# Retention readout scales computed with tokens on partitions and spread by TensorE, and weights prepared three units ahead in layer 0

## Chip, cores and metric

One core of one Trainium2 chip runs the whole network in one program. The metric is the device time of one execution in microseconds (us), lower is better. Engines are named as in the profile: PE is the matrix engine (TensorE), DVE the vector engine (VectorE), ACT the scalar engine (ScalarE), POOL is GpSimd, SP issues most transfers (SyncE).

## What is computed

A two-layer backbone over 512 tokens (256 context tokens, 256 latent tokens), model width 1024, all in float32. Layer 0 is a four-head bidirectional retention mixer followed by a gated convolutional feed-forward block; layer 1 is an RG-LRU mixer with the same kind of feed-forward block. What the change touches is the readout of one retention head:

```
def head_groupnorm(y, gain):
    mu = mean(y, axis=-1);  var = mean((y - mu)**2, axis=-1)      # over the head's 512 value columns
    return (y - mu) * rsqrt(var + EPS) * gain

def readout(y, g):
    return (silu(g) * head_groupnorm(y, gn)) @ w_out
```

So each head needs one scale per token: 512 numbers 1/sqrt(var + eps).

## The kernel before, in words

**Layout.** Activations lie transposed: a tile has 128 features on the partitions and the 512 tokens in its columns. A head's value output is four tiles `av` (128 of the 512 value columns each), left in PSUM; the means are already taken out. A scale per token therefore has to multiply the columns of a tile, and stands in every partition of a 128x512 tile.

**Matrix products.** Each float32 product is made of three faster ones (`mm3`, lines 522 to 524): both operands are split into a high and a low part, and high times high, high times low, low times high are added up in PSUM. For a weight block the parts are `whi` and `wlo`, for an activation they are for instance `zhi` and `zlo`.

**Weights.** All weight blocks (128x128) stand in one stream in the order of their use, cut in units of eight blocks. A unit arrives as `raw` (one transfer of 512 KB, nine buffers), ACT rounds it to `whi` (line 420), DVE subtracts to make `wlo` (line 452). When the first block of unit u is about to be used, `blk` calls `prep_units(u + ahead)`: it issues the low parts up to unit u + ahead and the high parts up to unit u + ahead + 1, never more than five units (WBUFS) beyond the current one. `self.ahead` is 1, then 2 while `start` runs, stays 2 through the retention layer and the first feed-forward block, and is set to 3 where `lru` begins. Some units hold weights for layer 1, which are split early and written back to DRAM (`pre`, line 471 and 479; `kept`, the transfers on ACT's queue), or matrices of the modulation: ACT multiplies them by a strip (`ada`, `adap`, lines 576 and 579) and POOL adds the products up (line 580).

**What sets the order.** Each engine does its instructions in the order in which the program records them. Some work is recorded late on purpose: `defer` puts pieces in a queue, `tick(n)` records the next n of them between two products, `flush` all of them; `lag` records the low part of a split one split later.

**A head.** For head h: four products for q and k, each followed by the rotation `rope_split` (lines 902 to 907: one copy on ACT, five instructions on DVE); for heads 1 and 2 then `ret_out(h-1)`, the output product of the head before (units of `ret_out` weights); a gate product; the scores; v (`ret_v`: per 128 tokens a mean `vm`, then `vhi` by ACT at line 961 and `vlo` by DVE at line 962); more gate products; `ret_av`, which leaves the four `av` tiles and `gacc`, the sum of their squares (`gsq`); then the readout. `ret_stats` makes the scale: one product of a tile of ones with `gacc` sums over the partitions and leaves the variance in all of them (`gst`, 128x512), ACT takes the square root (`sd`), DVE the reciprocal (`rstd`, line 679). `ret_z` makes four tiles z = av * gain * scale * silu(g) (`zt`, lines 1007 and 1008) and splits them (`zhi` on ACT, line 544, `zlo` on DVE, line 545), in five deferred pieces. For head 0 `ret_stats` stands after the first q/k product of head 1, for the others ahead of the last gate product. So the readout of heads 0, 1 and 2 is made while the q/k products of the next head run, and that of head 3 while `ret_out(2)` runs.

Of the kernel before, what the change touches and what calls it, by code (L numbers as in the profile page):

```python
# [7 lines left out]
F32 = mybir.dt.float32  # L8
F32R = mybir.dt.float32r
AF = mybir.ActivationFunctionType  # L10
ALU = mybir.AluOpType

P = 128
D = 1024
KD = D // P
NT = 512
# [40 lines left out]
def qk_cols(h):  # L57
    return [2 * h, 2 * h + 1, 8 + 2 * h, 8 + 2 * h + 1]
# [128 lines left out]
class Buf:  # L187


    def __init__(self, kind="s"):  # L190
        self.kind, self.n, self.t = kind, 0, None
# [105 lines left out]
class Net:  # L297
    def __init__(self, ctx, tc, wpk, xt, cv, par, cst, out):
        self.tc, self.nc, self.out = tc, tc.nc, out
        self.d_w, self.d_x, self.d_c, self.d_par, self.d_cst = wpk, xt, cv, par, cst  # L300
        self.cp = ctx.enter_context(tc.tile_pool(name="cp", bufs=1))
        self.wp = ctx.enter_context(tc.tile_pool(name="wp", bufs=WBUFS))
        self.gp = ctx.enter_context(tc.tile_pool(name="gp", bufs=1))
        self.pp = ctx.enter_context(tc.tile_pool(name="pp", bufs=8, space=bass.MemoryType.PSUM))
        self.nslot = 54
        self.uid = 0
        self.raw, self.units = {}, {}
        self.nload = self.nunit = self.nlo = self.pos = self.npast = 0
        self.held, self.ahead, self.spread, self.umode = None, 0, "A", {}
        self.auto = True  # L310
        self.piece_of = {p[1] // 16: i for i, p in enumerate(PIECES) if p[0] == "blk"}
        self.bg, self.lagq, self.due, self.now = deque(), deque(), [], 0
        self.ada_ps, self.ada_acc, self.adaq, self.ada_rate = {}, {}, deque(), 4
        self.ada_done, self.ada_sum = set(), {}
        self.preq, self.keepq = deque(), deque()
        self.dp = ctx.enter_context(tc.tile_pool(name="dp", bufs=1, space=bass.MemoryType.DRAM))
        self.kept = {}

# [674 lines left out]
        self.gacc = acc  # L993

    def ret_stats(self):
        ps = self.ps(name="gst")
        self.nc.tensor.matmul(ps, self.ones_v, self.gacc, start=True, stop=True)
        self.grs = self.rstd_of(ps, NT)

    def ret_z(self, h):  # L1000

        nc = self.nc
        zs, av, sg, rs = [], self.av, self.avsg, self.grs

        def first(c):
            t = self.slot(name="zt")
            nc.vector.scalar_tensor_tensor(t, av[c], self.pc("gn", 4 * h + c), rs, ALU.mult, ALU.mult)  # L1007
            nc.vector.tensor_tensor(t, t, sg[c], ALU.mult)
            hi = self.slot(dt=F32R, name="zhi")
            lo = self.slot(dt=F32R, name="zlo")  # L1010
            return t, hi, lo

        def step(c):
            if c:
                t, hi, lo = prev.pop()
                self.split(t, hi, lo)
                zs.append((hi, lo))
            if c < 4:
                prev.append(first(c))

        prev = []
        self.defer(*[lambda c=c: step(c) for c in range(5)])
        return zs

    def ret_out(self, h, zs):
# [89 lines left out]
    def retention(self):  # L1115
        self.hpos = {}
        self.setup()
        a = self.const([P, KD, 2], name="amul")
        hl = {}
        pss = self.start(a, hl)  # L1120
        zs = None
        for h in range(HEADS):
            self.sg = []
            if h == 0:
                qk = [self.rope_split(pss[j], j % 2) for j in range(4)]
                self.silu_g(pss[4])
                self.silu_g(pss[5])
                self.ret_g(h, hl, 2)
                self.decay(0)
            else:  # L1130
                qk = []
                for j, c in enumerate(qk_cols(h)):
                    ps = self.gemm("ret_in", range(KD), c, lambda k: [(0, hl[k])], NT)
                    if h == 1 and j == 0:
                        self.ret_stats()
                        zs = self.ret_z(0)
                    self.tick(2)
                    qk.append(self.rope_split(ps, j % 2))
                self.flush()
                if h < 3:  # L1140
                    self.ret_out(h - 1, zs)
                else:
                    zprev = zs
                self.ret_g(h, hl, 0)
            self.qk = (qk[:2], qk[2:])
            if h == 0:
                self.ret_v(h, hl)
                self.flush()
                self.ret_scores()
                self.ret_g(h, hl, 3)  # L1150
                self.ret_av()
                self.decay(1)
            else:
                self.flush()
                self.ret_scores()
                self.ret_v(h, hl)
                self.ret_g(h, hl, 1)
                self.ret_av()
                self.ret_g(h, hl, 2)
                if h < 3:  # L1160
                    self.decay(h + 1)
            if h:
                self.ret_stats()
                self.ret_g(h, hl, 3)
                zs = self.ret_z(h)
        self.ret_out(2, zprev)
        self.flush()
        self.need("f0")
        self.stats_begin()
        a = self.make_amul(self.const([P, KD, 2], name="amul"), 0, "norm_ffn")  # L1170
        for m in range(2):
            ps = self.gemm("ret_out", range(12, 16), m, lambda k: [(0, zs[k - 12])], NT)
            for s in range(2):
                self.residual(ps[:, s * NS:(s + 1) * NS], 0, 2, m, s)
                self.stats_add(m, s)
        self.hl = {}
        dst = lambda k, s: [t[:, s * NS:(s + 1) * NS] for t in self.hwide(k, self.hl)]
        return self.staged_out("ret_out", range(12, 16), range(2, KD), lambda k: zs[k - 12], 0, 2,
                               lambda s: self.norm_steps(0, "norm_ffn", a, s, dst))
# [611 lines left out]
```

## Time and profile before

| | |
|---|---|
| Device time, three runs | 1222.65, 1226.3, 1227.6 us (median 1226.3) |
| The profiled execution's own time | 1223.15 us |
| Span of its program in the trace | 1221.4 us |
| PE busy | 1186.3 us, 97% of the span |
| DVE, ACT, POOL busy | 892.5, 731.9, 360.0 us |
| PE idle for a low part of weights (line 452) | 18.5 us in nine times, the longest 6.0 us |

The profile is one execution. Busy PE time counts every matrix product from its issue to its modelled end, so 97% says that PE seldom has nothing to do; it does not say that its products run at full speed. The column PEclk of the views by stretch gives the clock that was granted to PE: 1.00 is 2.4 GHz, 0.50 is 1.2 GHz.

### The profile page before, as it was taken

How to read it: one execution, taken by the hardware profiler on the slowest of the kernel's cores; microseconds unless marked ns; L12 is line 12 of the kernel's file. 1: busy time of each engine (PE TensorE's matmuls, PEld its weight loads, DVE VectorE, ACT ScalarE, POOL GpSimd, SP SyncE). 2: the span in 40 equal slices, each digit the busy share in tenths (PEclk: the TensorE clock that was granted, in tenths of full speed). 3: DMA queues.
4: the chain of work that ended last, by engine and by line, in shares of the span. 5: the costliest groups of instructions: out<-in, count | busy, mean ns of one | idle time of the engine just before them, and what ended most of it. 6: DMA issues, size and time to landing. Idle time of an engine off the chain costs nothing.

```text
span 1221.4 us, 18028 instructions
## 1 busy us (share of the span) xinstructions
PE 1186.3 (97%) x6768; PEld 1010.2 (83%) x6768; DVE 892.5 (73%) x1285; ACT 731.9 (60%) x1100; POOL 360.0 (29%) x238
## 2 busy tenths in 40 slices
PE   9999799999979999999999999999999999999997
PEld 5678688778868889877878888789988788999996
DVE  5665996896596598599945676754658877988743
ACT  5465566765753545987643656542497956666542
POOL 0000555746370012798733435360000001000010
PEclk9999899999989999999999999999999999999999
DMA  9975479758566482445688645654586994655631
GB/s 334 339 253 216 182 238 318 250 193 310 208 224 212 145 319 100 143 154 191 215 313 268 222 153 203 231 196 159 162 313 204 327 333 162 193 187 183 195 107 35
DMA packets 79160, 265.38 MB, mean 217 GB/s; under 512 B 9312, under 2 KB 13024, under 8 KB 79072
## 3 DMA queue, kind: packets, MB, share of 16 engines
q1 hardware_dynamic: 66976, 221.75, 54.0%
q10 hardware_dynamic: 12096, 42.47, 8.9%
q8 instruction: 53, 0.87, 0.3%
q14 instruction: 35, 0.29, 0.1%
HBM read 219.62 MB, written 42.99 MB: 215 GB/s over the span
## 4 chain that ended last, share of the span: by engine, by line
PE 78%; DVE 12%; ACT 3%; DMA 3%; issue 2%; SPq 1%; DVEq 0%; ACTq 0%
PE ps L522 22%; PE ps L524 22%; PE ps L523 22%; DVE wlo L452 3%; PE ps L946 2%; PE ps L947 2%; PE ps L948 2%; DVE rstd L679 1%; ACT adap L579 1%; DVE fzlo L545 1%; PE av L524 1%; PE av L523 1%; PE av L522 1%; DVE zt L1007 1%; PE ps L1639 1%
## 5 line engine op out<-in xcount | busy, mean ns | idle before, releaser
L580 POOL TENSOR_TENSOR ada<-ada,adap 128x512 f32<-128x512 f32 x196 | 324.2, 1679 | 365.5 <-ACT adap L579 232.4
L524 PE MATMUL ps<-hhi,wlo 128*128 128x512 f32 (+1 forms) x640 | 245.6, 384 | 11.2 <-DVE wlo L452 11.2
L522 PE MATMUL ps<-hhi,whi 128*128 128x512 f32 (+1 forms) x640 | 248.7, 389 | 0.0
L523 PE MATMUL ps<-hlo,whi 128*128 128x512 f32 (+1 forms) x640 | 244.2, 382 | 0.0
L665 POOL TENSOR_TENSOR sq<-sq,sq 128x256 f32<-128x256 f32 x29 | 32.4, 1127 | 472.9 <-ACT sq L659 382.9
L523 PE MATMUL ps<-hx,whi 128*128 128x256 f32 x592 | 168.1, 284 | 0.4 <-DVE hx L698 0.2
L522 PE MATMUL ps<-hx,whi 128*128 128x256 f32 x592 | 168.3, 284 | 0.2 <-ACT hx L697 0.2
L524 PE MATMUL ps<-hx,wlo 128*128 128x256 f32 x592 | 167.5, 283 | 0.0
L524 PEld LDWEIGHTS ps<-hhi,wlo 128*128 128x128 f32 x640 | 121.6, 190 | 37.4 <-DVE wlo L452 14.5
L522 PEld LDWEIGHTS ps<-hhi,whi 128*128 128x128 f32 x640 | 121.7, 190 | 31.6 <-issue 6.5
L523 PEld LDWEIGHTS ps<-hlo,whi 128*128 128x128 f32 x640 | 121.7, 190 | 22.9 <-issue 1.0
L522 PEld LDWEIGHTS ps<-hx,whi 128*128 128x128 f32 x592 | 113.5, 192 | 4.2 <-issue 2.5
L523 PEld LDWEIGHTS ps<-hx,whi 128*128 128x128 f32 x592 | 113.5, 192 | 1.2 <-DVE hx L698 0.8
L524 PEld LDWEIGHTS ps<-hx,wlo 128*128 128x128 f32 x592 | 113.5, 192 | 0.0
L1190 DVE SCALAR_TENSOR_TENSOR cv<-ps,par,cv 128x510 f32<-128x510 f32 (+1 forms) x88 | 53.9, 613 | 61.7 <-ACT cv L1187 61.7
L1187 ACT ACTIVATE cv<-ps,par 128x512 f32<-128x512 f32 (+1 forms) x88 | 58.7, 670 | 65.8 <-PE ps L524 64.9
L522 PE MATMUL ps<-fzhi,whi 128*128 128x512 f32 (+1 forms) x198 | 72.7, 367 | 0.0
L524 PE MATMUL ps<-fzhi,wlo 128*128 128x512 f32 (+1 forms) x198 | 72.4, 365 | 0.0
L523 PE MATMUL ps<-fzlo,whi 128*128 128x512 f32 (+1 forms) x198 | 72.4, 365 | 0.0
L708 DVE SCALAR_TENSOR_TENSOR xc<-ps,mod,xc 128x256 f32<-128x256 f32 x48 | 23.0, 479 | 54.5 <-PE ps L524 54.4
L524 PE MATMUL ps<-zhi,wlo 128*128 128x512 f32 (+1 forms) x152 | 55.7, 366 | 7.4 <-DVE wlo L452 7.4
L1191 DVE SCALAR_TENSOR_TENSOR cv<-ps,par,cv 128x510 f32<-128x510 f32 (+1 forms) x88 | 54.2, 616 | 3.1
(791 smaller groups left out, 2786.4 us busy)
## 6 DMA issues: line engine op xcount, KB each, us to landing
kept<-pre ACTq DMA_DIRECT2D x40, 512.0 KB, 5.7
whi<-kept SPq DMA_DIRECT2D x40, 512.0 KB, 4.3
wlo<-kept SPq DMA_DIRECT2D x40, 512.0 KB, 5.5
ak<-wpk SPq DMA_DIRECT2D x32, 256.0 KB, 6.3
xc<-xt SPq DMA_DIRECT2D x4, 256.0 KB, 3.7
x<-xt SPq DMA_DIRECT2D x4, 256.0 KB, 5.2
xst<-xhi SPq DMA_DIRECT2D x16, 64.0 KB, 3.8
cst<-cst SPq DMA_DIRECT2D x3, 192.0 KB, 5.1
```

Of the source, the lines that this page charges most:

```text
L452: self.eng(e).tensor_tensor(d[q, o:n], r[q, o:n], hi[q, o:n].bitcast(F32), ALU.subtract)
L522: mm(ps, w[0], x[0], start=start, stop=False)
L523: mm(ps, w[0], x[1], start=False, stop=False)
L524: mm(ps, w[1], x[0], start=False, stop=stop)
L580: nc.gpsimd.tensor_tensor(acc[i, s], acc[i, s], t, ALU.add)
L665: nc.gpsimd.tensor_tensor(self.acc[s], self.acc[s], sq, ALU.add)
L946: mm(pss[t], xh, wh, start=k == 0, stop=False)
L947: mm(pss[t], xh, wl, start=False, stop=False)
L948: mm(pss[t], xl, wh, start=False, stop=k == KD - 1)
L1187: nc.scalar.activation(acc, ps[:, :n], AF.Identity, scale=w(1), bias=self.pc("fcb", layer * 44 + f))
L1190: nc.vector.scalar_tensor_tensor(a3[:, :, 1:], p3[:, :, :NS - 1], w(0), a3[:, :, 1:], ALU.mult, ALU.add)
L1191: nc.vector.scalar_tensor_tensor(a3[:, :, :NS - 1], p3[:, :, 1:], w(2), a3[:, :, :NS - 1], ALU.mult, ALU.add)
```

## The change

The scale of a head is made with a token per partition. Four products take a 128-token chunk of `gacc` as the stationary operand and one column of ones as the moving one, and leave the variances as 128x4; ACT's square root and DVE's reciprocal work on 128x4 (`gsd`). A new function, `spread_scale`, brings the 512 scales back into all partitions: four products take a column of `gsd`, repeated 128 times, as the stationary operand and the identity as the moving one (`gb`, 128x512 in PSUM), and ACT copies the result to SBUF (`grs`). It stands as one more deferred piece ahead of the five of `ret_z`. And `self.ahead` is set to 3 at the beginning of the head loop.

```diff
     def ret_stats(self):
-        ps = self.ps(name="gst")
-        self.nc.tensor.matmul(ps, self.ones_v, self.gacc, start=True, stop=True)
-        self.grs = self.rstd_of(ps, NT)
+        nc = self.nc
+        ps = self.ps([P, 4], name="gst")
+        for j in range(4):
+            nc.tensor.matmul(ps[:, j:j + 1], self.gacc[:, j * P:(j + 1) * P], self.ones_v[:, 0:1], start=True, stop=True)
+        self.gsd = self.gp.tile([P, 4], F32, tag="gs", name=f"gsd{self.nhead}", bufs=2)
+        nc.scalar.activation(self.gsd, ps, AF.Sqrt, bias=self.eps)
+        nc.vector.reciprocal(self.gsd, self.gsd)
+        self.nhead += 1
+
+    def spread_scale(self, sd):
+        ps = self.ps(name="gb")
+        for j in range(4):
+            self.nc.tensor.matmul(ps[:, j * P:(j + 1) * P], sd[:, j:j + 1].to_broadcast([P, P]), self.cc("ident"),
+                                  start=True, stop=True)
+        rs = self.slot(name="grs")
+        self.nc.scalar.copy(rs, ps)
+        return rs
...
-        zs, av, sg, rs = [], self.av, self.avsg, self.grs
+        zs, av, sg, sd, rs = [], self.av, self.avsg, self.gsd, []
...
-            nc.vector.scalar_tensor_tensor(t, av[c], self.pc("gn", 4 * h + c), rs, ALU.mult, ALU.mult)
+            nc.vector.scalar_tensor_tensor(t, av[c], self.pc("gn", 4 * h + c), rs[0], ALU.mult, ALU.mult)
...
-        self.defer(*[lambda c=c: step(c) for c in range(5)])
+        self.defer(lambda: rs.append(self.spread_scale(sd)), *[lambda c=c: step(c) for c in range(5)])
...
         pss = self.start(a, hl)
+        self.ahead = 3
         zs = None
         for h in range(HEADS):
```

Where the engines' orders move, at three places.

DVE before, the end of head 0's readout, during the q/k products of head 1 (rawN is a unit of weights; the last `zlo` is what `ret_out(0)` needs of its fourth block on):

```order
L906 TENSOR_TENSOR qklo_1315<-ps_1250,qkhi_1314 128x256
L907 TENSOR_TENSOR ra_1316<-ra_1316,rb_1317 128x256
L452 TENSOR_TENSOR wlo_1329<-raw24a,whi_1260 128x1024
L545 TENSOR_TENSOR zlo_1306<-zt_1302,zhi_1305 128x512
L617 TENSOR_TENSOR mod_170<-adat_1356,par_89 128x4 x4
L545 TENSOR_TENSOR zlo_1313<-zt_1309,zhi_1312 128x512
L903 TENSOR_TENSOR ra_1385<-ps_1324,cst_556 128x256
```

DVE with the change, at the same place:

```order
L453 TENSOR_TENSOR wlo_1365<-raw24b,whi_1281 128x1024
L546 TENSOR_TENSOR zlo_1338<-zt_1334,zhi_1337 128x512
L1023 SCALAR_TENSOR_TENSOR zt_1405<-av_1165,par_89,grs_1261 128x512
L1024 TENSOR_TENSOR zt_1405<-zt_1405,sg_1116 128x512
L546 TENSOR_TENSOR zlo_1345<-zt_1341,zhi_1344 128x512
L904 TENSOR_TENSOR ra_1414<-ps_1356,cst_556 128x256
L905 TENSOR_TENSOR rb_1415<-ps_1356,cst_558 64x256
L906 TENSOR_TENSOR rb_1415<-ps_1356,cst_558 64x256
L907 TENSOR_TENSOR qklo_1413<-ps_1356,qkhi_1412 128x256
L908 TENSOR_TENSOR ra_1414<-ra_1414,rb_1415 128x256
L453 TENSOR_TENSOR wlo_1427<-raw26a,whi_1363 128x1024
L546 TENSOR_TENSOR zlo_1409<-zt_1405,zhi_1408 128x512
```

Before, one rotation less and the low parts up to raw24a stood ahead of the last `zlo`; now the third rotation of head 1 and the low parts of raw24b and raw26a stand ahead of it too, while those of raw22b and raw21b have moved ahead of the first `zt`.

ACT before, the scale of head 0:

```order
L420 CAST whi_1191<-raw22b 128x1024
L677 ACT_TABLE_LOAD
L677 ACTIVATE sd_1221<-gst_1219,eps_178 128x512
L607 COPY adarow_1061<-ada_677 128x512
L471 CAST pre_1227<-raw21b 128x1024
L544 CAST zhi_1232<-zt_1229 128x512
```

ACT with the change, the scale of head 0 and its copy after the spreading:

```order
L421 CAST whi_1208<-raw24a 128x1024
L1003 ACT_TABLE_LOAD
L1003 ACTIVATE gsd_1241<-gst_1236,eps_178 128x4
L577 ACTIVATE ada_1204<-raw23a,strip_183 128x512
L577 ACTIVATE ada_1205<-raw23a,strip_183 128x512
L580 ACTIVATE adap_1246<-raw23a,strip_183 128x512
L580 ACTIVATE adap_1249<-raw23a,strip_183 128x512
L488 DMA kept_1252<-pre_1005 128x1024
L489 DMA kept_1252<-raw21a 128x1024
L1013 COPY grs_1261<-gb_1256 128x512
```

Between the square root and the copy, ACT now has four products of the modulation and two transfers to issue.

ACT before, the split of v of head 1:

```order
L961 ACTIVATE vhi_1925<-ps_1733,vm_1913 128x512
L961 ACTIVATE vhi_1928<-ps_1734,vm_1916 128x512
L961 ACTIVATE vhi_1932<-ps_1735,vm_1919 128x512
L961 ACTIVATE vhi_1936<-ps_1736,vm_1922 128x512
L471 CAST pre_1953<-raw34b 128x1024
L487 DMA kept_1956<-pre_1910 128x1024
L488 DMA kept_1956<-raw34a 128x1024
L487 DMA kept_1959<-pre_1953 128x1024
L488 DMA kept_1959<-raw34b 128x1024
L420 CAST whi_1964<-raw38a 128x1024
```

ACT with the change, at the same place:

```order
L421 CAST whi_1921<-raw38a 128x1024
L577 ACTIVATE ada_1902<-raw36a,strip_183 128x512
L577 ACTIVATE ada_1903<-raw36a,strip_183 128x512
L580 ACTIVATE adap_1951<-raw36a,strip_183 128x512
L580 ACTIVATE adap_1954<-raw36a,strip_183 128x512
L472 CAST pre_1957<-raw37a 128x1024
L962 ACTIVATE vhi_1971<-ps_1773,vm_1959 128x512
L962 ACTIVATE vhi_1974<-ps_1774,vm_1962 128x512
L962 ACTIVATE vhi_1978<-ps_1775,vm_1965 128x512
L962 ACTIVATE vhi_1982<-ps_1776,vm_1968 128x512
```

The rounding of raw38a and the work on raw36a and raw37a, which stood behind the four `vhi`, stand ahead of them.

## Rows read from the trace of the kernel before

**Rows 1.** The page, part 1: busy us, share of the span, instructions.

```profile
PE 1186.3 (97%) x6768; PEld 1010.2 (83%) x6768; DVE 892.5 (73%) x1285; ACT 731.9 (60%) x1100; POOL 360.0 (29%) x238
```

**Rows 2.** Waits of PE in 110:160, 245:255, 345:372, 500:585: total us, times, longest.

```profile
PE ps L524 <- DVE wlo L452: 6.2, 2, 6.0
...
PE ps L524 <- DVE wlo L452: 1.6, 2, 1.3
...
PE ps L524 <- DVE wlo L452: 7.0, 2, 4.0
...
PE ps L524 <- DVE wlo L452: 3.7, 3, 2.3
```

**Rows 3.** Windows: PE, PEld, DVE, ACT, POOL busy, PEclk, DMA share, GB/s.

```profile
142.00:150.00 8.00, 5.44 (x13) 4.16 (x14) 7.94 (x13) 5.34 (x10) 8.00 (x6) 0.50 0.52 183
...
152.00:160.00 8.00, 8.00 (x36) 6.30 (x35) 7.81 (x15) 3.43 (x6) 3.23 (x3) 1.00 0.47 143
...
364.00:368.00 4.00, 4.00 (x11) 3.14 (x10) 3.94 (x8) 0.32 (x2) 0.51 (x1) 0.50 0.74 256
```

**Rows 4.** Timeline of PE, products without the three-part split: start, us.

```profile
119.28 1.02 PE L997 MATMUL gst<-gsq,ones_v 128*128 128x512 f32 x2
...
131.04 0.96 PE L613 MATMUL adat<-cst,adarow 128*128 128x24 f32 x8
```

**Rows 5.** Groups of DVE by form: busy us, mean ns, idle us ahead of them.

```profile
L679 DVE RECIPROCAL rstd<-sd 128x512 f32<-128x512 f32 x4 | 13.4, 3353 | 9.3 <-ACT sd L677 9.3
...
L617 DVE TENSOR_TENSOR mod<-adat,par 128x4 f32<-128x4 f32 x32 | 2.6, 153 | 6.9 <-PE adat L613 6.8
```

**Rows 6.** Timeline of ACT and DVE, readout of head 0.

```profile
120.39 1.28 ACT L677 ACT_TABLE_LOAD   x1 [0.84 <-PE gst L997]
121.68 0.69 ACT L677 ACTIVATE sd<-gst,eps 128x512 f32<-128x512 f32 x1
...
122.40 3.35 DVE L679 RECIPROCAL rstd<-sd 128x512 f32<-128x512 f32 x1 [2.10 <-ACT sd L677]
...
126.75 0.74 DVE L1007 SCALAR_TENSOR_TENSOR zt<-av,par,rstd 128x512 f32<-128x512 f32 x1
...
129.53 0.42 DVE L903 TENSOR_TENSOR ra<-ps,cst 128x256 f32<-128x256 f32 x1
...
131.52 1.22 DVE L452 TENSOR_TENSOR wlo<-raw22b,whi 128x1024 fp32r<-128x1024 f32 x1
...
134.36 2.31 DVE L479 TENSOR_TENSOR raw21b<-raw21b,pre 128x1024 fp32r<-128x1024 f32 x1
...
142.22 2.28 DVE L452 TENSOR_TENSOR wlo<-raw24a,whi 128x1024 fp32r<-128x1024 f32 x1
...
146.39 1.49 DVE L545 TENSOR_TENSOR zlo<-zt,zhi 128x512 fp32r<-128x512 f32 x1
```

**Rows 7.** Timeline of ACT and PE, split of v of head 1.

```profile
199.64 3.05 ACT L961 ACTIVATE vhi<-ps,vm 128x512 fp32r<-128x512 f32 x4 [3.71 <-DVE vm L955]
...
206.01 0.39 PE L522 MATMUL av<-phi,vhi 128*128 128x512 f32 x1
...
209.18 1.05 ACT L420 CAST whi<-raw38a 128x1024 fp32r<-128x1024 f32 x1 [5.55 <-PE av L524]
210.13 1.33 ACT L576 ACTIVATE ada<-raw36a,strip 128x512 f32<-128x512 f32 x2
```

**Rows 8.** Timeline of DVE and PE, end of the readout of head 1.

```profile
252.19 1.29 DVE L545 TENSOR_TENSOR zlo<-zt,zhi 128x512 fp32r<-128x512 f32 x2
...
254.28 0.39 PE L523 MATMUL ps<-zlo,whi 128*128 128x512 f32 x1
```

**Rows 9.** Timeline of DVE and PE, q/k products of head 3 with the readout of head 2.

```profile
343.17 0.75 DVE L1007 SCALAR_TENSOR_TENSOR zt<-av,par,rstd 128x512 f32<-128x512 f32 x1
...
371.26 0.39 PE L522 MATMUL ps<-qkhi,qkhi 128*128 128x512 f32 x1
...
371.37 0.98 DVE L545 TENSOR_TENSOR qklo<-ra,qkhi 128x256 fp32r<-128x256 f32 x2
```

More of the change, by code (lines that the diff above doesn't have):

```diff
@@ L315, in __init__ @@
         self.preq, self.keepq = deque(), deque()
+        self.nhead = 0
         self.dp = ctx.enter_context(tc.tile_pool(name="dp", bufs=1, space=bass.MemoryType.DRAM))
```

## The prediction, made before the changed kernel was run

> **What bounds the kernel now.** I began with the page: PE is busy for 1186.3 of 1221.4 us [rows 1], so whatever is gained must come from PE's few gaps, and whatever is added to PE counts in full where PE has no gap. Next the waits of PE, stretch by stretch, where one reads who ended each gap. All of the gaps that matter here end on a low part of weights made by DVE, and four stretches hold all 18.5 us: the readouts of heads 0, 1 and 2 (6.2, 1.6 and 7.0 us) and the start of the first feed-forward block (3.7 us) [rows 2]. Then the windows around the longest gap: after it, PE ran at a granted clock of 0.50, that is 1.2 GHz, and did 13 products in 5.44 us, 0.42 us each; at 1.00 it did 36 in 8.00 us, 0.22 us each [rows 3]. The slow stretch holds 14 products, so such a gap costs 14 x 0.20 = 2.8 us more than its length. The window 364:368 shows 0.50 again, after the gaps of head 2. Last the timelines of DVE around the readouts: in 142:150 DVE was busy 7.94 of 8 us, and it is DVE's queue, not one instruction, that is late.
>
> The profiled execution took 1223.15 us, 3.15 below the median of the three runs. I make the sum against 1223.15 and add 3.15 at the end.
>
> **What the change costs on PE.** The old `gst` was one product in two records, 1.02 us; four small float32 products with the same number of records as the new ones took 0.96 us [rows 4]. Four products with one moving column should thus cost what the old one did, +0.05 us. The four spreading products move 128 columns, between the 24 of those four and the 512 of `gst`: at least 0.96; as an upper bound, a record of 512 columns takes 1.02 / 2 = 0.51 and one of 24 takes 0.96 / 8 = 0.12, in proportion 0.20 for 128, 1.6 for eight. I take 0.95 to 1.0, near the 24-column row, because the small products seem bound by their weight loads. So +1.0 us per head, +4.2 in all, but only where PE does not wait for DVE behind it. For head 0 the spreading follows the scale at once in PE's order, so PE must also wait for ACT's square root (at most the 0.69 of the old one [rows 6]) and DVE's reciprocal (128x4; another 128x4 operation takes 0.153 [rows 5]): some 1.2 us, which the later wait for DVE swallows.
>
> **What DVE is spared.** Four reciprocals of 3.35 us, and 9.3 us of idling ahead of them [rows 5]. The new reciprocal is 0.15 to 0.2 us. This is the intended gain: the first `zt` can begin earlier and more low parts be done ahead. Stretch by stretch:
>
> **Head 0 to 1: +3.1 us.** ACT's table load no longer waits for `gst` [rows 6], so the square root ends near 121.1. Ahead of the copy ACT then has two `ada` and two `adap`, 2 x 1.33 = 2.65 us [rows 7], so the scale lies in SBUF at 121.1 + 2.65 + 0.6 = 124.35 (the copy at most the 0.69 of a 128x512 square root), and the first `zt` begins near 124.4 where it was 126.75: 2.35 earlier. From there to the end of the last `zlo` at 147.88 DVE was busy without a gap for 21.1 us [rows 6]. In the new order the subtractions of raw22b (1.22) and raw21b (2.31) are out of this stretch, -3.5; but one more rotation (5 x 0.42 = 2.1) and the low parts of raw24b and raw26a (2 x 2.3) have come in, because the pieces stand one tick later and the lead is longer [rows 6]. 21.1 - 3.5 + 2.1 + 4.6 = 24.3, which ends at 148.7; with more of it beside POOL's additions I take 149.6 (bounds 146 and 151). Before, PE met the last `zlo` at 148.1 with no wait left. It will now pass this point 1.5 us later, and what is still to be made up at half clock grows from 6 of the 14 slow products to all: 8 x 0.2 = 1.6. Together +3.1, bounds -1 and +6. The products added are inside, since PE waits behind them.
>
> In [rows 6] the same subtraction takes 1.22 us (raw22b) and 2.28 us (raw24a), while POOL was busy in all of 142:150 [rows 3]. The Trainium skill, "SBUF — State Buffer", section Terms, says of the port pair that DVE and GpSimd share that "the loser **fully blocks**"; the trace agrees with a DVE instruction standing still for a POOL addition, at 2.28 against 1.22. By that sentence alone all DVE work moved into POOL's bursts would cost about double, and the stretch above would end nearer its later bound.
>
> **Split of v of head 1: +2 us.** In the new order the four `vhi` stand behind the rounding of raw38a, two `ada`, two `adap` and one `pre`: 1.05 + 2.65 + 1.05 = 4.75 us of ACT. Before, the first `vhi` began at 199.64, and PE asked for it at 206.01: 6.4 us to spare, of which 4.75 are used up without harm. But raw38a must have landed too, and its rounding ran at 209.18 [rows 7]. If its buffer comes free as much earlier as the lead grows, the wait is 0; if it comes as late as 206, PE waits about 4 us. I take the middle.
>
> **Head 1 to 2: +0.8 us.** The last `zlo` ended at 253.48 (252.19 + 1.29), and PE used it at 254.28 after a wait of 1.6 [rows 2, 8]. The first `zt` can begin some 2.8 us earlier, since the long reciprocal and its square root are gone, but again a rotation (2.1) and a low part (2.3) have come ahead of the last `zlo`: 253.48 - 2.8 + 4.4 = 255.1. That is 0.8 past 254.28. Bounds -1.6 (no wait at all) and +3.
>
> **Head 2 to 3: -0.6 us.** From the first `zt` at 343.17 to the last `qklo` at 372.35 DVE was busy for 29.2 us; the scores of head 3, which need those `qklo`, began at 371.26, just in time [rows 9]. Two subtractions move ahead into DVE's idle time, and the scale comes about 1.2 us earlier: I reckon the last `qklo` at 342.0 + 26.5 = 368.5. So the 7.0 us of waits for low parts become one wait of about the same length ahead of the scores, which then run at half clock at first (2.8). PE gets through some 0.6 us earlier than now. Bounds -4 and +3.
>
> **Head 3: +1.0 us.** PE has no wait there before [rows 2], so the added products count in full.
>
> **First feed-forward block: -3.7 us.** One more unit of lead is eight blocks, 24 products of 0.22 = 5.3 us, more than all three waits there [rows 2, 3]. Bounds -3.7 and -1, since DVE may still be behind.
>
> Sum: 3.1 + 2 + 0.8 - 0.6 + 1.0 - 3.7 = +2.6; 1223.15 + 2.6 = 1225.8 in the terms of the profiled execution, and with 3.15 about 1228.9; I say 1228. A measurement of this kernel tells 0.5%, 6.1 us, from no change; this is within it.
>
> **The rivals.**
>
> *A, the readouts come free (faster).* If the last `zlo` of head 0 is done before PE needs it, the gap, and the slow clock behind it, go. In full: -18.5 - 2.8 behind head 0 - 2.8 behind head 2 + 4.2 of added products = -19.9, 1206; with half of the waits left, 1216. For it: DVE is spared 3.35 us right ahead of each chain, and ACT's table load moves away from it. Against: the rotation and the low parts that come ahead of the last `zlo` are longer than what goes.
>
> *B, v is split late (slower).* If the raw unit that ACT now rounds ahead of `vhi` lands no earlier than before, the four `vhi` of heads 1 to 3 start late, PE stands at `av` for about 4 us a head, and on two of them at least the slow clock follows: 3 x 4 in place of the 2 in my sum, +10, 1239. It decides from the point where the first `vhi` of head 1 starts more than 6.4 us after the mean is there, plus what PE itself is late. Against: earlier low parts free the raw buffers earlier, so the transfers start earlier too.
>
> *C, PE's own work decides.* If DVE's relief only moves waits about, what is left is +4.2: 1230.5. The Trainium skill says in "Perfetto Trace Analysis", section Identifying the Most-Contended Engine, that the engine to optimize first is the most contended one; that speaks against giving PE work in order to relieve DVE, and the trace agrees as far as PE's 97% goes.
>
> *D, the lead does not come about.* If the buffers (nine raw, five units) hold the preparation where it is, the feed-forward block keeps its 3.7 us, head 1's split stays as it is, and the rotation and low parts still move: 2.6 + 3.7 - 2 = +4.3, about 1230.
>
> **How the numbers follow.** My sum 0.27 (its own bounds, terms taken as independent: 1222 to 1234), C 0.08 and D 0.07, A 0.33, B 0.25. The range reaches from the nearer half of A to most of B: 1211 to 1239; it leaves out the best of A, 1 in 10, and the worst of B, 1 in 10. Faster by over 0.5% is A, 0.33; slower is B, 0.25; the rest, 0.42, is no change.
>
> **What would show it.** In the profile after: PE's wait in the feed-forward start gone (my step) or still 3.7 us (D); the first `zt` of head 0 about 2 us earlier in the same place of the program, and the last `zlo` not; PE's waits of head 0 now on `zlo` instead of a weight's low part; in head 2 to 3 a wait on `qklo` in front of the scores; a wait on `vhi` or `vlo` at head 1's `av` of 0 to 4 us (over 4, or at all three heads: B). If the waits of the readouts sum to under 5 us and the clock stays at 1.00, A is right and my count of DVE's new order was wrong. The spreading products over 1.6 us a head would make every term too small.

## The result and the profile after

The changed kernel took 1238.9 us (median of four runs, 1236.4 to 1240.7) against 1226.5 before: ratio 1.0105, 95% interval 1.0076 to 1.0134. It is slower by 1%. I had forecast 1228, no change that can be measured.

Part 1 of the page of the changed kernel (its span is 1234.6 us, its own time 1236.4), to be held against [rows 1]:

```profile
PE 1194.2 (97%) x6824; PEld 1018.2 (82%) x6824; DVE 882.6 (71%) x1285; ACT 732.3 (59%) x1104; POOL 348.5 (28%) x238
```

DVE has 9.9 us less to do and PE 7.9 more, and still the whole is 13 us longer. The waits of PE between 60 and 700 us (total, times, longest), which answer to [rows 2]:

```profile
PE ps L524 <- DVE zlo L546: 12.4, 4, 5.4
PE ps L524 <- DVE qklo L546: 3.2, 2, 2.5
PE ps L523 <- ACT fzhi L545: 2.1, 1, 2.1
PE ps L523 <- DVE vlo L963: 1.6, 1, 1.6
PE ps L524 <- DVE fzlo L546: 1.4, 1, 1.4
PE gb L1010 <- DVE gsd L1004: 1.2, 1, 1.2
PE av L525 <- DVE vlo L963: 1.2, 1, 1.2
PE ps L525 <- DVE wlo L453: 0.6, 2, 0.4
...
```

The change did what it says: the waits for low parts of weights (`wlo`), 18.5 us before, are down to 0.6. In their place PE waits for the low and high parts of activations (`zlo`, `qklo`, `fzlo`, `fzhi`, `vlo`), 22 us of them. To see where the time went I took the difference of the start times of the same product in both traces; for the first gate product of head 2, behind `ret_out(1)`, in the kernel before:

```profile
273.77 0.39 PE L522 MATMUL ps<-hhi,whi 128*128 128x512 f32 x1
```

and in the changed one:

```profile
287.60 0.50 PE L523 MATMUL ps<-hhi,whi 128*128 128x512 f32 x1
```

so it is 13.83 us late there. Such differences, taken at eight such products and the first product of v of head 0 (where both stand at 71.4 to 71.5), give what each stretch gained (-) or lost (+):

| stretch (start in the kernel before) | change | my term |
|---|---|---|
| v of head 0, readout of head 0, `ret_out(0)` (71.5) | +4.4 | +3.1 |
| rest of head 1, its split of v (169.2) | +3.3 | +2 |
| readout of head 1 and `ret_out(1)` (221.0) | +6.3 | +0.8 |
| rest of head 2 (273.8) | -0.9 | 0 |
| readout of head 2, scores of head 3 (326.2) | -4.6 | -0.6 |
| head 3, its readout, `ret_out(2)` (375.4) | +0.8 | +1.0 |
| last output product, feed-forward block up (462.8) | -3.3 | -3.7 |
| first down products (599.4) | +6.7 | 0 |

They sum to 12.7; 0.9 comes later. Two rows are shifted by work that only changed its row: with a lead of three, a group of PE products of the modulation (`ada`, 1.06 us) stands one matrix product earlier, which makes 1.2 us of the +3.3 and about 1 us of the -0.9. Three of the runs below have the order of the changed kernel up to their own edits, and give 3.8 to 5.7 for the first row, 2.4 to 3.3 for the second, 5.8 and 6.1 for the third (in the two that leave that stretch as it is): a row of one trace is good to about 1 us.

Two stretches hold as much as the whole loss. First, the readout of head 1. DVE, PE and POOL there, in the changed kernel:

```profile
239.51 1.05 PE L1010 MATMUL gb<-cst,gsd 128*128 128x128 f32 x8
...
241.22 0.75 DVE L1023 SCALAR_TENSOR_TENSOR zt<-av,par,grs 128x512 f32<-128x512 f32 x1 [5.85 <-ACT grs L1013]
...
259.11 6.55 POOL L581 TENSOR_TENSOR ada<-ada,adap 128x512 f32<-128x512 f32 x4 [4.51 <-ACT adap L580]
...
259.16 1.50 DVE L908 TENSOR_TENSOR ra<-ra,rb 128x256 f32<-128x256 f32 x1
260.58 2.29 DVE L453 TENSOR_TENSOR wlo<-raw43a,whi 128x1024 fp32r<-128x1024 f32 x1
262.79 1.74 DVE L546 TENSOR_TENSOR zlo<-zt,zhi 128x512 fp32r<-128x512 f32 x1
...
264.59 0.79 PE L524 MATMUL ps<-zlo,whi 128*128 128x512 f32 x1 [5.40 <-DVE zlo L546]
```

The reciprocal was done at 233, but PE came to the spreading only at 239.51, behind the first q/k product of head 2. DVE idled for 5.85 us, the first `zt` began at 241.22, and at the end a low part of a later weight unit stands ahead of the last `zlo`, for which PE waits 5.40 us. Both run inside a burst of POOL's additions. In the kernel before, the last `zlo` ended at 253.48 [rows 8], as such a burst began:

```profile
253.31 2.57 POOL L580 TENSOR_TENSOR ada<-ada,adap 128x512 f32<-128x512 f32 x2 [9.56 <-ACT adap L579]
```

Second, the first down product of the changed kernel:

```profile
610.21 2.25 DVE L453 TENSOR_TENSOR wlo<-raw93a,whi 128x1024 fp32r<-128x1024 f32 x1
...
612.38 0.68 DVE L546 TENSOR_TENSOR fzlo<-cv,fzhi 128x512 fp32r<-128x512 f32 x1
...
613.12 0.50 PE L524 MATMUL ps<-fzlo,whi 128*128 128x512 f32 x1 [1.36 <-DVE fzlo L546]
...
615.99 0.79 PE L523 MATMUL ps<-fzhi,whi 128*128 128x512 f32 x1 [2.14 <-ACT fzhi L545]
```

Before, PE had no wait here. Two windows (columns as in [rows 3]) show the stretch up to here, and what follows the two waits:

```profile
520.00:600.00 80.00, 79.41 (x352) 64.13 (x351) 78.59 (x65) 64.11 (x97) 78.06 (x47) 1.00 0.54 173
...
616.00:621.00 5.00, 5.00 (x11) 3.62 (x12) 4.96 (x7) 2.78 (x3) 0.00 (x0) 0.50 0.38 95
```

DVE is busy for 78.59 of 80 us, with POOL busy beside it for 78.06; then the clock stands at 0.50. 3.5 us of waits cost 6.65. The kernel before has a DVE that is just as full there, and paid at the start of the block instead:

```profile
520.00:600.00 80.00, 78.33 (x345) 63.30 (x346) 79.03 (x63) 62.02 (x94) 76.46 (x45) 1.00 0.55 180
```

### The profile page after: what moved, and what is told of

Same layout as the page of the kernel before. It is cut to its first block, busy times and chain, and to the rows that moved or that the text cites. A ratio compares the mean times of both kernels' runs of the same rounds, so it can differ in the third digit from the quotient of the medians.

```text
span 1234.6 us, 18144 instructions
## 1 busy us (share of the span) xinstructions
PE 1194.2 (97%) x6824; PEld 1018.2 (82%) x6824; DVE 882.6 (71%) x1285; ACT 732.3 (59%) x1104; POOL 348.5 (28%) x238
## 4 chain that ended last, share of the span: by engine, by line
PE 69%; DVE 15%; ACT 6%; DMA 6%; issue 3%; SPq 0%; ACTq 0%; DVEq 0%
PE ps L523 20%; PE ps L524 20%; PE ps L525 20%; DVE wlo L453 5%; ACT adap L580 2%; PE ps L947 1%; PE ps L948 1%; PE ps L949 1%; ACT whi L421 1%; DVE zlo L546 1%; PE av L525 1%; DVE fzlo L546 1%; PE av L524 1%; PE av L523 1%; DMA kept<-raw15b 1%
## 5 line engine op out<-in xcount | busy, mean ns | idle before, releaser
L581 POOL TENSOR_TENSOR ada<-ada,adap 128x512 f32<-128x512 f32 x196 | 315.5, 1635 | 374.7 <-ACT adap L580 365.1
L523 PE MATMUL ps<-hhi,whi 128*128 128x512 f32 (+1 forms) x640 | 246.0, 384 | 1.6 <-DVE vlo L963 1.6
L525 PE MATMUL ps<-hhi,wlo 128*128 128x512 f32 (+1 forms) x640 | 242.8, 379 | 0.6 <-DVE wlo L453 0.6
L666 POOL TENSOR_TENSOR sq<-sq,sq 128x256 f32<-128x256 f32 x29 | 29.5, 1026 | 488.9 <-ACT sq L660 488.5
L524 PE MATMUL ps<-zlo,whi 128*128 128x512 f32 (+1 forms) x152 | 56.6, 373 | 12.4 <-DVE zlo L546 12.4
```

The costliest lines, as they stand in the source:

```text
L523: mm(ps, w[0], x[0], start=start, stop=False)
L524: mm(ps, w[0], x[1], start=False, stop=False)
L525: mm(ps, w[1], x[0], start=False, stop=stop)
L581: nc.gpsimd.tensor_tensor(acc[i, s], acc[i, s], t, ALU.add)
L666: nc.gpsimd.tensor_tensor(self.acc[s], self.acc[s], sq, ALU.add)
```

## The experiments

My theory 1 after the result: DVE's work is nearly the same as before, its queue is in order, and so a low part made earlier is made ahead of something that PE needs sooner; and the scale, though cheap on DVE now, sits in PE's queue behind a product. Rival 2: the loss is the work added to PE, and the rest is harmless. Ratios below are to runs of the kernel before, with 95% intervals.

**The lead alone.** In the kernel before:

```diff
         pss = self.start(a, hl)
+        self.ahead = 3
```

> The kernel before with the lead of three units alone; the scales are made as before. Theory 1 (DVE's work is the same, a longer lead only sets low parts of later weights ahead of the low parts of activations that PE needs sooner): the split of v of heads 0 and 1 (+1.7 and +2), the start of the feed-forward block (-3.4) and its first down product (+6.6) show here as in the changed kernel, and PE's waits in the readouts are on zlo or qklo instead of wlo; in sum +5 to +11 over before, 1231 to 1237. Rival 2 (the lead is harmless, the loss is the work added to PE): the waits for wlo go and nothing takes their place, -3 to -12, 1214 to 1223.

1236.3 us, ratio 1.0097 (1.0078 to 1.0117). Its waits of PE:

```profile
PE ps L523 <- DVE zlo L545: 8.4, 3, 6.5
PE ps L523 <- DVE qklo L545: 6.1, 1, 6.1
PE ada L594 <- POOL ada L580: 2.8, 2, 1.6
PE av L522 <- ACT vhi L961: 2.2, 1, 2.2
PE ps L522 <- ACT fzhi L544: 2.1, 1, 2.1
PE ps L522 <- DVE vlo L962: 1.8, 1, 1.8
...
PE ps L523 <- DVE fzlo L545: 1.3, 1, 1.3
...
```

Without any work added to PE the loss is nearly the whole one, and most of the waits are on the same tiles. By stretches: head 1 with its split of v +5.0 (1.2 of it the moved product again), readout of head 1 +3.5, feed-forward block up -3.3, down +7.2. Rival 2 falls for the lead.

**The new scales alone.** The changed kernel without the line above.

```diff
         pss = self.start(a, hl)
-        self.ahead = 3
```

> The changed kernel with the lead of two units as before; only the new scales are in. Theory 1: the scale of heads 1 to 3 now waits in PE's queue behind the first q/k product, so the first zt of head 1 starts 3 us later than before although the long reciprocal is gone; +1 us of PE work a head; at head 0 to 1 and 1 to 2 waits of PE grow by 2 to 5 us, no new wait in the feed-forward block; 1229 to 1236. Rival 2 (only the added PE work counts): +1.2 us at each of four places and no other change, 1231, with the readout waits as before or shorter.

1230.1 us, ratio 1.0038 (1.0022 to 1.0055). Added to the 0.97% of the lead alone this makes 1.35%, against 1.05% (0.76 to 1.34) for both together; the intervals leave open whether the two losses overlap. The stretch with the scale of head 0 costs +2.5 and the readout of head 1 +2.2; the feed-forward block is as before to within 0.03 in both of its stretches. The first `zt` of head 1:

```profile
239.54 0.75 DVE L1023 SCALAR_TENSOR_TENSOR zt<-av,par,grs 128x512 f32<-128x512 f32 x1 [4.51 <-ACT grs L1013]
```

DVE stood idle for 4.51 us ahead of it, for a scale whose reciprocal was long done. The same `zt` in the kernel before:

```profile
237.87 0.74 DVE L1007 SCALAR_TENSOR_TENSOR zt<-av,par,rstd 128x512 f32<-128x512 f32 x1
```

It begins 1.7 us later with the new scales, where I had expected 3, and PE's waits grew by 1.7 us at head 0 and 1.8 at head 1, less than the 2 to 5 of theory 1. The total, 1230 where both said about 1231, does not tell theory 1 from rival 2; the next run does.

**The spreading recorded at once.** The changed kernel, with the spreading and its copy where the pieces are queued:

```diff
-        self.defer(lambda: rs.append(self.spread_scale(sd)), *[lambda c=c: step(c) for c in range(5)])
+        rs.append(self.spread_scale(sd))
+        self.defer(*[lambda c=c: step(c) for c in range(5)])
```

> The changed kernel, with the spreading recorded at once where the pieces of the readout are queued (for heads 1 to 3 ahead of the next q/k product on PE, and each piece of the readout one place earlier again) instead of as one more queued piece. Theory 1: the first zt of head 1 starts 4 to 6 us earlier than in the changed kernel and PE's wait of 5.4 us there shrinks to 0 to 2 with full clock behind it: 4 to 8 us less than the changed kernel, 1231 to 1235. Rival 2: place doesn't matter, as the same work is on PE: within 1.5 us of the changed kernel, 1239.

1224.0 us, ratio 0.9998 (0.9986 to 1.0010): 1.07% less than the changed kernel, about 13 us, with the same work on every engine. That is more than the 4 to 8 I expected. The readout of head 1 fell from +6.3 to +1.4, as expected; but that of head 0 (from behind its scale to the end of `ret_out(0)`) also fell, from +0.1 to -5.1, where the scale's place on PE is the same in both, and that of head 2 from -4.6 to -9.3. So it isn't only the spreading that counts, but also the places of the five pieces behind it. Rival 2 falls here too.

**The two moves told apart.** As the last, with an empty piece ahead of the five:

```diff
+        rs.append(self.spread_scale(sd))
-        self.defer(lambda: rs.append(self.spread_scale(sd)), *[lambda c=c: step(c) for c in range(5)])
+        self.defer(lambda: None, *[lambda c=c: step(c) for c in range(5)])
```

> The kernel with the spreading at once (lead three), with an empty piece put ahead of the five pieces of each readout, so that zt and zlo stand where the changed kernel has them while the spreading itself stays ahead of the q/k product. Tells the two moves of the spreading apart. If the scale's place behind the q/k product on PE was what counted: as with the spreading at once, 1222 to 1226. If the place of the pieces, one tick later behind another rotation and another low part on DVE, was what counted: near the changed kernel, 1235 to 1240. Theory 1 expects both: the 5.4 us wait of head 0 with its slow clock comes back (there the scale's place is the same in both), that of head 1 mostly not; 1229 to 1233.

1234.9 us, ratio 1.0093 (1.0078 to 1.0108); a little above what I expected. The 5.4 us wait of head 0 is back, and its readout goes from -5.1 to +1.7: 6.8 us for one tick (5.1 beside the changed kernel, whose pieces stand in the same place). At head 1 the stretch is +4.0, so about 2.7 of its 4.9 us are the pieces' place and 2.2 the spreading's. The place of the pieces was the bigger part.

**The new scales at once, with the old lead.**

```diff
         pss = self.start(a, hl)
-        self.ahead = 3
...
-        self.defer(lambda: rs.append(self.spread_scale(sd)), *[lambda c=c: step(c) for c in range(5)])
+        rs.append(self.spread_scale(sd))
+        self.defer(*[lambda c=c: step(c) for c in range(5)])
```

> The kernel with the spreading at once, but with the lead of two units as before: the new scales alone, at the place that costs least. Theory 1 (place of the pieces decides the readouts, the lead of three costs at the split of v and at the first down product): no wait at head 0's v, no wait at the first down product, waits of 3.7 us at the start of the feed-forward block as before, readouts of heads 0 and 1 with waits of under 3 us each; 1221 to 1228. Rival 3 (it is the longer lead together with the early scales that gives 1224): the wlo waits of head 0 and 2 come back in full, 6 and 7 us with slow clock behind, and with 4 us of added PE work it takes 1228 to 1232.

1218.4 us, ratio 0.9961 (0.9949 to 0.9973): faster than both kernels. Run once more for the last two experiments:

> The kernel with the spreading at once and a lead of two once more, beside these two on the same chip, as the value they are compared with: 1217 to 1220 by either theory.

1217.7 us, ratio 0.9958 (0.9943 to 0.9974). The spreading and the first `zt` of head 1 in this second run, and its waits of PE from 60 to 700:

```profile
224.83 1.16 PE L1010 MATMUL gb<-cst,gsd 128*128 128x128 f32 x8
...
230.40 0.75 DVE L1023 SCALAR_TENSOR_TENSOR zt<-av,par,grs 128x512 f32<-128x512 f32 x1 [1.13 <-ACT grs L1013]
```

```profile
PE ps L525 <- DVE wlo L453: 7.1, 3, 3.8
PE gb L1010 <- DVE gsd L1004: 1.3, 2, 1.2
PE av L525 <- DVE vlo L963: 1.1, 2, 0.7
PE st L672 <- ACT sq L660: 0.8, 1, 0.8
PE ps L524 <- DVE zlo L546: 0.7, 1, 0.7
```

The first `zt` of head 1 begins 7.5 us sooner than in the kernel before, 4.5 by PE's own time (PE is 3.0 us ahead there), and the waits for `wlo` are 7.1 instead of 18.5 us with the lead of two: a shorter DVE queue ahead of the readout was enough. Rival 3 falls. Beside the run with a lead of three, 0.9998 against 0.9961, the longer lead costs 0.37%, about 4.5 us, even with the pieces in their good place.

**The lead ended within the feed-forward block.** In the changed kernel, ahead of the last but one feature tile of the first half:

```diff
             for m in ks:
+                if m == FA - 2:
+                    self.ahead = 2
```

> The changed kernel, with the lead set back to two units at the last but one feature tile of the first half of layer 0's feed-forward block. Theory 1: at the first down product DVE then has one low part (2.3 us) less ahead of the last fzlo and fzhi; the waits of 1.4 and 2.1 us there and the slow clock behind them go in whole or in large part: 3 to 6.6 us less than the changed kernel, 1232 to 1236, with the start of the block still without waits. Rival 2 (the wait there comes from something else, the added work or the shift of everything ahead): 1239.

1234.4 us, ratio 1.0082 (1.0064 to 1.0101), 2.8 us less than the changed kernel by the ratios, whose intervals overlap: the total alone does not show a gain. The waits at the first down product:

```profile
PE ps L523 <- ACT fzhi L545: 1.8, 1, 1.8
PE ps L524 <- DVE fzlo L546: 0.5, 1, 0.5
PE ps L525 <- DVE wlo L453: 0.2, 1, 0.2
```

2.5 us of waits are left of 3.5, and the stretch still costs +4.9 instead of +6.7: the direction of theory 1, but less than the 3 us that it asked for at least. That fits a backlog of DVE larger than one low part; this run does not show it.

**POOL's additions taken out of the feed-forward block.** In the changed kernel; `light` is set from the third feature tile of the feed-forward block on, and most of layer 1's modulation is left out:

```diff
-                nc.gpsimd.tensor_tensor(acc[i, s], acc[i, s], t, ALU.add)
+                n = 1 if self.light else NT
+                nc.gpsimd.tensor_tensor(acc[i, s][:, :n], acc[i, s][:, :n], t[:, :n], ALU.add)
```

> The changed kernel, with POOL's additions of the modulation cut to one column of 512 from the third feature tile of layer 0's feed-forward block on (most of layer 1's modulation is thereby left out). Theory 1 (in the feed-forward block DVE is busy all the time, slowed by POOL's additions, so a longer lead only moves its backlog from the start of the block to its first down product): low parts take 1.2 us instead of 2.3, the waits of 1.4 and 2.1 us at the first down product and the slow clock behind them go; 5 to 8 us less than the changed kernel, 1231 to 1234. Rival 4 (the order with the longer lead makes the wait, however fast DVE is): the waits at the down product stay, 1238.

1230.1 us, ratio 1.0055 (1.0040 to 1.0069), 0.5% or 6 us less than the changed kernel. PE has no wait at all from 500 to 700 us; the down stretch falls from +6.7 to 0.0. The window that answers to the one above:

```profile
520.00:600.00 80.00, 80.00 (x358) 65.29 (x357) 56.44 (x70) 70.33 (x107) 24.71 (x48) 1.00 0.60 201
```

The same program order with a DVE that is busy for 56 of 80 us instead of 79 makes no wait. It is DVE's backlog beside POOL, not the order alone; the lead chose where PE pays for it (with a lead of two both stretches are as before). Rival 4 falls.

**The same during the readout of head 1.** The additions are cut while the q/k products of head 2 are recorded (the same line; `light` is set ahead of their loop for head 2 and cleared behind it), and a part of the modulation is left out:

```diff
                 qk = []
+                self.light = h == 2
                 for j, c in enumerate(qk_cols(h)):
...
                 self.flush()
+                self.light = False
```

> The changed kernel, with POOL's additions of the modulation cut to one column of 512 while the q/k products of head 2 are recorded (a part of the modulation is thereby left out). In the changed kernel five DVE instructions ahead of the end of the last zlo of head 1 (two low parts, two zlo, one rotation step) each take about 1.1 us longer than the shortest of their kind, all beside POOL's additions. If that is what makes the wait of 5.4 us: the wait falls to under 1 us, the slow clock behind it goes, 6 to 8 us less than the changed kernel: 1230 to 1233. If DVE's order alone makes it: the wait stays at 4 to 5.4 us, 1237 to 1239.

1231.1 us, ratio 1.0067 (1.0050 to 1.0085): 4.7 us less by the ratios, 7.7 in the stretch itself (+6.3 to -1.5). PE has no wait from 220 to 290 us. The last rotation step, low part and `zlo` there:

```profile
259.01 0.42 DVE L909 TENSOR_TENSOR ra<-ra,rb 128x256 f32<-128x256 f32 x1
259.35 1.22 DVE L453 TENSOR_TENSOR wlo<-raw43a,whi 128x1024 fp32r<-128x1024 f32 x1
260.49 0.68 DVE L546 TENSOR_TENSOR zlo<-zt,zhi 128x512 fp32r<-128x512 f32 x1
```

They take 0.42, 1.22 and 0.68 us where they took 1.50, 2.29 and 1.74. So this wait can be removed in either of two ways, by the order or by POOL: the late start put DVE's work beside a burst of additions.

**Where the longer lead should pay.** On top of the spreading at once, a lead of three from behind head 0's v to the end of `ret_out(2)`, two elsewhere:

```diff
                 self.ret_v(h, hl)
+                self.ahead = 3
...
         self.ret_out(2, zprev)
         self.flush()
+        self.ahead = 2
```

> The kernel with the spreading at once, with the lead of three units only from behind the split of v of head 0 to the end of the third output product, two elsewhere. Theory 1: no wait for vlo at head 0's v (2.4 us), no waits at the first down product (3.4 us with slow clock) but the 3.7 us at the start of the feed-forward block again; 1 to 4 us less than the kernel with the spreading at once: 1220 to 1223. Rival: DVE is behind anyway, what goes there comes back at the next wait: 1224.

1223.0 us, ratio 0.9995 (0.9984 to 1.0005), the same as with three units everywhere. The waits at head 0's v and at the down product are gone, but 3.9 us at head 0's `zlo`, 3.2 at head 1's `vhi` and 2.4 at the feed-forward start are there instead. By the ratios this is 0.4 us less and not the 1 to 4 of theory 1: the rival was right. And with a lead of three only from the readout of head 2 on, to the end of `ret_out(2)`:

```diff
+            if h == 2:
+                self.ahead = 3
             if h:
                 self.ret_stats()
```

> The kernel with the spreading at once and a lead of two, with three units only from the readout of head 2 to the end of the third output product. Theory 1 (a longer lead pays where DVE is idle ahead of the place that asks for it, and costs where DVE is behind): the 3.8 us wait for a low part in head 2 to 3 and its slow clock go, as in the kernels with a lead of three there, which gained 9 to 11 us over that stretch against 3.6 with a lead of two; 4 to 6 us less than with a lead of two throughout: 1212 to 1215. Rival: what goes there comes back at the scores or at the split of v of head 3: 1217 to 1220.

1218.8 us, ratio 0.9965 (0.9951 to 0.9978); with the lead taken back ahead of the first gate product of head 3:

```diff
                     zprev = zs
+                    self.ahead = 2
```

> As the kernel with three units from the readout of head 2 on, but back to two before the first gate product of head 3. Theory 1: the gain of that stretch is made there and kept, and the low parts of head 3 and of the third output product cost what they cost with a lead of two: within 1.5 us of the other, 1211 to 1215. If the longer lead in head 3 itself carried the gain: 1216 to 1219.

1219.5 us, ratio 0.9967 (0.9955 to 0.9979). Neither gains on the lead of two. I had expected 1212 to 1215 and 1211 to 1215, and was wrong: in the first of them PE no longer waits 3.8 us for `wlo` there, but at the scores:

```profile
PE ps L524 <- DVE qklo L546: 5.9, 1, 5.9
```

The large gains in this stretch that I had read off the other kernels came with a PE that arrived there 6 to 9 us later than in the kernel before. In the kernel at once, PE comes to the scores 11.4 us later than here, DVE to the last `qklo` that they need only 5.7 us later: DVE had caught up. A stretch's gain is not its own alone.

## Why the prediction was wrong, point by point

**The step that failed first** is the one for head 1 to 2: "253.48 - 2.8 + 4.4 = 255.1". By PE's own time (PE came to `ret_out(1)` 6.4 us late, 1.0 of it for the spreading just ahead, so 5.4 are taken off) the first `zt` began at 235.8, near my 235.1. But the last `zlo` ended at 264.53, by the same time at 259.1, 4.0 later than I said: from the first `zt` to there DVE needed 23.3 us and not 20.0. I had priced the rotation and the low part that come ahead of the last `zlo`, and not the POOL additions that the other instructions of this longer chain run into; with them cut, the wait was gone. Nor had I counted the slow clock behind such a wait, 2.8 us by my own figure for head 0. And I took it as given that the scale of heads 1 to 3 waits behind a q/k product in PE's queue: DVE idled for 5.85 us there, and with the spreading ahead of that product, and the pieces a tick earlier, the +6.3 of this stretch fell to +1.4, and with the lead of two to -1.4. Together +6.3 where I said +0.8.

**The step that was missing** is the first down product. I took -3.7 for the start of the feed-forward block (measured -3.3, so right in itself) and said that DVE "may still be behind" only as a lower bound for this gain. DVE is busy without a gap up to the down product; what PE does not wait at the start it waits at the end, and there the slow clock comes on top: +6.7. The run with light POOL work shows it.

**The split of v.** Its mechanism was right, its place incomplete. Of head 1's +3.3, 1.7 us are lost at v (I said 2); most of the rest is the product of the modulation that moved into this row. Head 0 lost another 1.7 (1.7 to 3.9 in the four traces of this order), which I had not looked at: `vhi` waited there behind the rounding of a unit whose transfer had not landed. In the changed kernel:

```profile
98.12 1.05 ACT L421 CAST whi<-raw22a 128x1024 fp32r<-128x1024 f32 x1 [12.09 <-DMA raw22a<-wpk]
99.07 1.04 ACT L472 CAST pre<-raw21a 128x1024 fp32r<-128x1024 f32 x1
100.02 1.26 ACT L962 ACTIVATE vhi<-ps,vm 128x512 fp32r<-128x512 f32 x2
```

That is rival B's mechanism, at heads 0 and 1 instead of 1 to 3, at 1.7 us each instead of 4. Its time, 1239, was met, and with it the edge of my range, but mostly by the two steps above: that is luck.

**What held.** The cost of the products: the four with one moving column took 0.95 to 1.05 us, the spreading 1.05 to 1.16, about as priced; PE's wait for the first reciprocal was 1.17 (I said 1.2). Head 0 to 1 lost 2.6, its 4.4 less the 1.7 at v, where I said 3.1, with a wait of 5.4 us for the last `zlo` and the slow clock behind it. Head 3 lost 0.8 (+1.0 said). Head 2 to 3 was of the right kind, a wait for `qklo` at the scores, but gained 4.6 instead of 0.6, just outside its bounds.

**The rivals.** A did not come to pass with this order, though the run at once with the old lead shows that a part of it was to be had. C named no more than the cost of the products, and D did not come to pass either: the waits of the feed-forward start went. The Trainium skill, "Perfetto Trace Analysis", section Identifying the Most-Contended Engine, says to optimize the most contended engine first; I had read that as speaking against giving PE work for DVE's sake. Here the runs differ from that reading: PE got the same products in the kernel at 0.9961 as in the one at 1.0038. Where they stood decided, not that they were added. The sentence that I cited from the Trainium skill, "SBUF — State Buffer", section Terms, is borne out as far as these runs reach: with POOL's additions cut, the same DVE instructions fell from 2.29 to 1.22 and from 1.74 to 0.68 us, by about the same 1.1 us for both sizes, as if each stood still for a while and then ran at its own speed. I had read it as about double; a fixed loss weighs more on the small instructions, which I had left at their short times.

**What stays open.** Why the longer lead costs 0.37% with the pieces in their good place is read from the stretches of one trace each (v of heads 0 and 1, the readouts, the down product). No place was found where it pays: three kernels with the lead of three in a part of the layer were no faster than the lead of two throughout. What part of the +6.3 is the slow clock was not measured apart.

## What to carry to other kernels

When an engine with a queue in order is full, preparing more ahead need not remove a wait: here it moved it to whatever now stood behind the preparation, and a slow clock behind the new wait made it dearer (3.5 us of waits at the down product cost 6.65; the 3.7 us that went at the start of the block had been worth 3.3). Before moving a step to another engine, find where it will stand in that engine's queue, and follow the whole chain there and back; here one tick for the pieces and one product for the spreading decided between 0.4% faster and 0.4% slower. And undo the parts of a change one by one: its good half was hidden by its other half and by its place.

## What the runs showed of the hardware that I had not expected

Small float32 products cost by their number much more than by their moving columns: four (eight records) took 0.95 to 1.05 us with 1 moving column, 0.96 with 24 [rows 4], 1.05 to 1.16 with 128.

A DVE instruction that runs beside POOL's additions loses about the same time whatever its size. Between the changed kernel and the one with the additions cut, the three that stand one behind the other ahead of the end of head 1's last `zlo` lost 1.08 us (128x256), 1.07 (128x1024) and 1.06 (128x512).

The first 71 us vary between executions of the same program: the first product of head 0's v stood at +3.4 us in one profiled execution of the kernel at once with the old lead and at 0.0 in the other, against the kernel before. The stretches above are therefore counted from that product on.
